# x for the sums on the GpSimd queue behind a pause of the weight sums, and the first dilated head beside them

## The chip, the core and the metric

The kernel runs on one core of a Trainium2 chip. Such a core has a matrix engine (TensorE, PE in the profile; its weight loads are PEld), a vector engine (VectorE, DVE), an engine for activations (ScalarE, ACT), a general engine (GpSimd, POOL) and an engine that mainly issues transfers (SyncE, SP). Each works through its own list of instructions in order and waits for the others by semaphores. SP and POOL each issue transfers (DMAs); the profile calls SP's queue `hardware_dynamic` (q1) and POOL's `software_dynamic` (q0). The metric is the device time of one execution in microseconds (us); smaller is better.

## What is computed

One layer of a decoder in float32 on x (512 tokens, 1024 channels). With `proj = x @ w_in`, cut into queries, keys, values and gates of three branches:

```python
o_da = diff_attention(...)            # 4 heads
o_sb = stick_breaking_attention(...)  # 8 heads
o_dl = dilated_attention(...)         # 3 groups x 4 heads: (window, dilation) = (128,1), (512,4), (2048,16)
g = jax.nn.sigmoid(gates).reshape(B, S, N_BRANCHES, D)
merged = (g[:, :, 0] * (o_da @ w_branch_da) + g[:, :, 1] * (o_sb @ w_branch_sb)
          + g[:, :, 2] * (o_dl @ w_branch_dil))
m = merged @ w_out
x = layer_norm(DEEPNORM_ALPHA * x + m, ln1_g, ln1_b)
c = jnp.square(relu(x @ w_up)) @ w_down
ple = jax.nn.sigmoid(x @ w_ple_gate) * (p @ w_ple)
x = layer_norm(DEEPNORM_ALPHA * x + c + ple, ln2_g, ln2_b)
```

The three dilated groups of one head slot are joined by their softmax denominators, so a dilated head in the kernel handles one slot of all three groups.

## The kernel before

Every large product is made of three matmuls of rounded parts: a float32 tile is split in a high part (`h`, a cast on ScalarE, L213) and the rest (`l`, a subtraction on VectorE, L215), and high x high, high x low and low x high are added up in PSUM. The weights come from HBM by SP in chunks of 512 KB (`raw`, seven buffers), are split into `wh` and `wl` (six buffers each), and are used by PE.

*Items.* The main stream is a list of items, each some 12 to 24 matmuls into one PSUM bank (`mm_bank`, two banks, or `at_bank`, six), and an eviction on ScalarE or VectorE when the next item has begun. Items 1 to 32 and 47 to 64 are projections (`t_item` and `v_items`; dl_v of group 0 is items 19 to 22, da_v 47 to 50), 65 to 72 the stick-breaking branch product (`branch_items(1)`), then gates, the other branches, `wout_items`, the layer norm and the MLP. Items 33 to 46 are the *value pair* (`value_pair`): the values of dilated groups 1 and 2 by a Strassen-like scheme with seven products, in the order 2, 1, 7, 6, 4, 5, 3, each in two halves r = 0, 1 of 12 matmuls. Half 0 of the first four or five products uses an `mm` bank, the others `at` banks. The scheme needs sums of weights and sums of x.

*Sums of weights* are made by the DMA engines alone, from HBM to HBM, with accumulating transfers issued on GpSimd (`sum_steps`, L1021; `vsum` for the value pair, `msum` for the gates, `bsum`, `gsum`, `usum`, `dsum` for later stages). How many steps an item emits is its `rate` x `size`, saved up as a credit (L1954 to L1960). A step waits for `marks[0]`, the fourth last entry of a list into which every split of a weight chunk (L218) and the evictions of `v_items` (L473) put their instruction; so a step runs no earlier than a VectorE instruction a few splits back. GpSimd issues in order: a step that waits holds all behind it.

*Sums of x* for the value pair come from `value_forms` (L345), a generator that begins at item 29: eight tiles `xr` of 256 KB are loaded on SP (L349), each after the last split emitted so far; VectorE then makes form 7 (L372), 6 (L365), 4 and 5 (L390), each split into high and low part (`split`, L239 on ScalarE, L240 on VectorE; u7h and u7l for form 7). `mixer_forms` (L513, begun at item 64) does the same for the gates, with eight loads in `load_xr` (L333).

*Heads.* Attention heads are generators too. `step()` (L1886), called once or twice in each item, moves every active head one `yield` on and starts waiting ones if PSUM banks suffice. Eight stick-breaking heads come first (`sb_head`), and only when none is active the first dilated head (`dil_head`, L1731). This makes logits of group 0 (matmuls L1749, bias and maximum L1752, exponent L1758), then of groups 1 and 2 (L1765, L1773, L1780), joins the denominators across rows (small matmuls L1790 and L1792 up to L1812, with an exponent L1807 on ScalarE), scales its maps (L1814, L1818), transposes them on PE (L1833, L1842) and multiplies them by the values (L1854, L1859). Head 0 waits with the whole of this until form 5 of `value_forms` is made (L1737), and takes two idle steps before its transposes (L1821).

Where an engine's instructions end up in its list is decided by a scheduler that goes by these dependences and the order of emission; engines run that list in order.

Of the kernel before, what the change touches and what calls it, by code (L numbers as in the profile page):

```python
# [55 lines left out]
def trunk(tc, a, out):  # L56
    nc = tc.nc
    es = ExitStack()
    with es:
# [14 lines left out]
        def slot(name, dt=F32):  # L74
            return big.tile([P, 512], dt, name=nm(name), tag="s", bufs=NSLOT)
# [63 lines left out]
        marks = deque(maxlen=4)  # L139
# [13 lines left out]
        def chunk(src, w):  # L153
            return chunk_of(load(src, w))
# [77 lines left out]
        items = []  # L232
# [14 lines left out]
        xt = a["xT"]  # L247
# [45 lines left out]
        def first_item():  # L293
# [19 lines left out]
            def ev(ps):  # L313
# [7 lines left out]
        vf = {p: [[(xh[k][:, 2 * th + r::4], xl[k][:, 2 * th + r::4]) for r in range(2)] for k in range(ks, ks + 4)]  # L321
              for p, ks, th in ((1, 0, 0), (2, 4, 0), (3, 4, 1))}
# [3 lines left out]
        def load_xr():  # L326

            r = {}
            for h in range(2):
                for th in range(2):  # L330
                    for kp in range(2):
                        t = slot("xr")
                        i = nc.sync.dma_start(t.rearrange("p (k t) -> p k t", k=2),  # L333
                                                xt[:, 4 * h + 2 * kp:4 * h + 2 * kp + 2, 256 * th:256 * th + 256])
                        tc.add_manual_dep(getattr(i, "ins", i), lows[-1].name, mybir.DependencyInfo(
                            mybir.DependencyClass.Sync, mybir.DependencyReason.DATA), reason="not ahead of time")
                        r[h, th, kp] = t
            return [[r[h, th, kp] for kp in range(2)] for h in range(2) for th in range(2)]
# [6 lines left out]
        def value_forms():  # L345

            xr = [slot("xr") for _ in range(8)]
            for k, t in enumerate(xr):
                i = nc.sync.dma_start(t, xt[:, k, :])  # L349
                tc.add_manual_dep(getattr(i, "ins", i), lows[-1].name, mybir.DependencyInfo(  # L350
                    mybir.DependencyClass.Sync, mybir.DependencyReason.DATA), reason="not ahead of time")

            def blk(kh, k, th):
                return xr[4 * kh + k].rearrange("p (t c) -> p c t", c=4)[:, 2 * th:2 * th + 2, :]

            def new():
                ts = [slot("fr") for _ in range(2)]
                return ts, [ts[k // 2].rearrange("p (k c t) -> p k c t", k=2, c=2)[:, k % 2] for k in range(4)]

            def parts(p, ts):  # L360
                form(vf, p, ts)
                vf[p] = [[(h[:, r * P:r * P + P], lo[:, r * P:r * P + P]) for r in range(2)] for h, lo in vf[p]]

            def neg_sub(o, i, j):
                nc.vector.scalar_tensor_tensor(o, i, -1.0, j, op0=OP.mult, op1=OP.subtract)  # L365

            for _ in range(WAIT):
                yield
            f7, o7 = new()
            with tc.issue_after(st["low"]):  # L370
                for k in range(4):
                    nc.vector.tensor_sub(o7[k], blk(1, k, 1), blk(0, k, 1))  # L372
            parts(7, f7)
            yield
            f6, o6 = new()
            with tc.issue_after(st["low"]):
                for k in range(4):
                    neg_sub(o6[k], o7[k], blk(0, k, 0))
            yield
            parts(6, f6)  # L380
            yield
            f4, o4 = new()
            for k in range(4):
                neg_sub(o4[k], o6[k], blk(1, k, 0))
            yield
            parts(4, f4)
            yield
            f1, o1 = new()
            for k in range(4):
                nc.vector.tensor_sub(o1[k], blk(0, k, 0), blk(0, k, 1))  # L390
            yield
            parts(5, f1)
            yield
# [53 lines left out]
        def v_items(nv, name, g):  # L447
            cs = [chunk(a["wv"][nv, c].rearrange("p k n -> p (k n)"), 1024) for c in range(4)]
            for tt in range(4):
                def mm(ps, tt=tt):  # L450
                    for k in range(8):
                        c = cs[k // 2]
                        s = slice((k % 2) * 512, (k % 2) * 512 + 512)
                        x1, x2 = xh[k][:, tt * P:tt * P + P], xl[k][:, tt * P:tt * P + P]
                        nc.tensor.matmul(ps, x1, c["h"][:, s], start=k == 0, stop=False)  # L455
                        nc.tensor.matmul(ps, x1, c["l"][:, s], start=False, stop=False)  # L456
                        nc.tensor.matmul(ps, x2, c["h"][:, s], start=False, stop=k == 7)  # L457
                        if k == 3:
                            yield

                def ev(ps, tt=tt):
                    if name == "sb_v":
                        v = [slot(name, F32R).rearrange("p (h two d) -> p h two d", two=2, d=64) for _ in range(2)]
                        pv = ps.rearrange("p (h d) -> p h d", d=64)
                        for i in range(2):
                            hs = slice(4 * i, 4 * i + 4)
                            nc.scalar.copy(v[i][:, :, 0, :], pv[:, hs, :])
                            nc.vector.tensor_sub(v[i][:, :, 1, :], pv[:, hs, :], v[i][:, :, 0, :].bitcast(F32))
                        V[name, g, tt] = v
                    else:  # L470
                        t = slot(name)
                        i = nc.vector.tensor_copy(t, ps)
                        marks.append(getattr(i, "ins", i))  # L473
                        marks.append(getattr(i, "ins", i))
                        V[name, g, tt] = t
                item(cs if tt == 3 else [], mm, ev, need=cs)
                items[-1]["rate"] = 2.5

        nt, nv = 2, 0
        order = main_order()  # L480
# [160 lines left out]
        def branch_items(i):  # L641
            for half in range(2):
                cs = [chunk(a["wb"][i - 1, half, c].rearrange("p k n -> p (k n)"), 1024) for c in range(2)]
                for tt in range(4):
                    def mm(ps, tt=tt, cs=cs):
                        q = slice(tt * P, tt * P + P)
                        for k in range(4):
                            c = cs[k // 2]
                            n = slice(k % 2 * 512, k % 2 * 512 + 512)
                            h, lo = oTs[4 * i + k]  # L650
                            nc.tensor.matmul(ps, h[:, q], c["h"][:, n], start=k == 0, stop=False)
                            nc.tensor.matmul(ps, h[:, q], c["l"][:, n], start=False, stop=False)
                            nc.tensor.matmul(ps, lo[:, q], c["h"][:, n], start=False, stop=k == 3)

                    def ev(ps, tt=tt, half=half):
                        if i == 1:
                            t = slot("b1")
                            nc.scalar.copy(t, ps)
                            merged[tt, half] = t
                            return  # L660
                        g = sg.pop((i, tt, half))
                        nc.vector.tensor_mul(g, g, ps)
                        nc.vector.tensor_add(merged[tt, half], merged[tt, half], g)

                    def pre(tt=tt, half=half):
                        sg[i, tt, half] = gate_sig(i, tt, half)
                    item(cs if tt == 3 else [], mm, ev, need=cs, bank=None if i == 1 else at_bank, size=0.5)
                    items[-1]["rate"] = 1.4
                    if i != 1:
                        items[-1]["pre"] = pre  # L670

# [93 lines left out]

        last_plain = len(items)
        for j, it in enumerate(items):
            it.setdefault("rate", 2.5 if j < 45 else 1.9)
        def first_gate(tt, half):
            g = gate_sig(1, tt, half)  # L770
            nc.vector.tensor_mul(merged[tt, half], merged[tt, half], g)
# [959 lines left out]
        def dil_head(hd):  # L1731
# [2 lines left out]

            while hd == 1 and ("dl_v", 1, 3) not in V:
                yield
            while hd == 0 and 5 not in vf:  # L1737
                yield
            q = [T["dl_q", 4 * g + hd] for g in range(3)]
            k = [T["dl_k", 4 * g + hd] for g in range(3)]  # L1740
            stt = one.tile([P, 2, 8], F32, name=nm("st"), tag="st", bufs=4)
# [76 lines left out]
                nc.vector.tensor_scalar(o, o, mxx[:, c:c + 1], None, op0=OP.mult)  # L1818
            yield

            for _ in range(2 if hd == 0 else 0):  # L1821
                yield

            src0 = {}
# [4 lines left out]
            for half in range(2):  # L1829
# [4 lines left out]
                t = slot("pt0")  # L1834
# [4 lines left out]
            for g in range(2):  # L1839
# [4 lines left out]
                t = slot("pt12")  # L1844
# [69 lines left out]
        for n, it in enumerate(items):  # L1914
# [63 lines left out]
            if n == ln2_at[0]:  # L1978

                i = nc.scalar.activation(small("rt", 1), ident[:, 0:1], AF.Sqrt)  # L1980
# [8 lines left out]
            ps = it["bank"]() if it["bank"] else mm_bank()  # L1989
# [113 lines left out]
```

## Time and profile before

| | us |
|---|---|
| runs of the kernel before | 1066.92, 1066.62, 1065.95; median 1066.62 |
| profiled execution | 1068.65, span of its instructions 1066.9 |

| engine | busy us | share of the span |
|---|---|---|
| PE | 1039.9 | 97% |
| PEld | 883.7 | 83% |
| DVE | 778.8 | 73% |
| ACT | 589.7 | 55% |
| POOL | 167.5 | 16% |

The profile is of one execution. A group's row has the source line, the engine, the operation, what it writes and reads, the count, and times. A row of the list of waits names the waiting instruction, what released it, the total, how often, and the longest. A row of the timeline has start, length, the instruction, and in brackets the idle time of its engine before it with the releaser. A row of the chain has start, length and what ran or was waited for. A window's row has the busy time of each engine in a stretch, the share of full clock that PE was granted, and the mean busy share of the 16 DMA engines. Line numbers are those of the kernel before; in the changed kernel they are one higher from L659 to L1736 and one lower from L1739 on.

### The profile page before, as it was taken

How to read it: one execution, taken by the hardware profiler on the slowest of the kernel's cores; microseconds unless marked ns; L12 is line 12 of the kernel's file. 1: busy time of each engine (PE TensorE's matmuls, PEld its weight loads, DVE VectorE, ACT ScalarE, POOL GpSimd, SP SyncE). 2: the span in 40 equal slices, each digit the busy share in tenths (PEclk: the TensorE clock that was granted, in tenths of full speed). 3: DMA queues.
4: the chain of work that ended last, by engine and by line, in shares of the span. 5: the costliest groups of instructions: out<-in, count | busy, mean ns of one | idle time of the engine just before them, and what ended most of it. 6: DMA issues, size and time to landing. Idle time of an engine off the chain costs nothing.

```text
span 1066.9 us, 15075 instructions
## 1 busy us (share of the span) xinstructions
PE 1039.9 (97%) x5462; PEld 883.7 (83%) x5462; DVE 778.8 (73%) x1392; ACT 589.7 (55%) x1006; POOL 167.5 (16%) x259
## 2 busy tenths in 40 slices
PE   9999999997799999999999999999999999999996
PEld 6887788876588888888888888888999989989885
DVE  6888667636865754878866786789677877877966
ACT  6666545514534544667672663585765565666641
POOL 0012312300020311101211122111211111111000
PEclk9999999998899999999999999999999999999999
DMA  8348977995494996837998998369999989989612
GB/s 311 115 159 260 216 214 231 303 303 148 136 287 123 280 269 200 233 113 261 277 351 261 340 313 288 115 206 325 303 334 339 337 275 328 301 290 289 196 39 80
DMA packets 76394, 260.09 MB, mean 244 GB/s; under 512 B 9144, under 2 KB 12104, under 8 KB 76320
## 3 DMA queue, kind: packets, MB, share of 16 engines
q0 software_dynamic: 32336, 116.21, 41.7%
q1 hardware_dynamic: 43408, 142.01, 36.8%
q8 instruction: 43, 0.70, 0.3%
q10 hardware_dynamic: 576, 0.92, 0.2%
q14 instruction: 31, 0.25, 0.1%
HBM read 256.98 MB, written 111.17 MB: 345 GB/s over the span
## 4 chain that ended last, share of the span: by engine, by line
PE 88%; DVE 4%; DMA 3%; ACT 2%; issue 2%; SPq 0%; POOL 0%; DVEq 0%; POOLq 0%
PE mm L87 9%; PE mm L89 9%; PE mm L88 9%; PE at L1211 4%; PE at L1212 4%; PE at L1213 4%; PE at L558 3%; PE at L560 3%; PE at L559 3%; PE mm L455 2%; PE mm L457 2%; PE mm L456 2%; DMA xr<-in_xT_dram 2%; PE at L89 1%; PE at L88 1%
## 5 line engine op out<-in xcount | busy, mean ns | idle before, releaser
L215 DVE TENSOR_TENSOR wl<-raw,wh 128x1024 fp32r<-128x1024 f32 x254 | 309.1, 1222 | 127.7 <-ACT wh L213 125.5
L213 ACT CAST wh<-raw 128x1024 fp32r<-128x1024 f32 x254 | 265.9, 1049 | 237.9 <-PE mm L88 127.2
L87 PE MATMUL mm<-xhT,wh 128*128 128x512 f32 x304 | 121.1, 398 | 0.0
L89 PE MATMUL mm<-xhT,wl 128*128 128x512 f32 x304 | 119.1, 392 | 0.0
L88 PE MATMUL mm<-xlT,wh 128*128 128x512 f32 x304 | 118.8, 391 | 0.0
L1211 PE MATMUL at<-wh,hh 128*128 128x512 f32 x188 | 73.7, 392 | 0.0
L1212 PE MATMUL at<-wl,hh 128*128 128x512 f32 x188 | 73.7, 392 | 0.0
L87 PE MATMUL mm<-x1hT,wh 128*128 128x256 f32 x256 | 73.6, 288 | 0.1
L1213 PE MATMUL at<-wh,hl 128*128 128x512 f32 x188 | 73.1, 389 | 0.0
L88 PE MATMUL mm<-x1lT,wh 128*128 128x256 f32 x256 | 72.2, 283 | 0.0
L89 PE MATMUL mm<-x1hT,wl 128*128 128x256 f32 x256 | 71.8, 283 | 0.0
L89 PEld LDWEIGHTS mm<-xhT,wl 128*128 128x128 f32 x304 | 57.1, 188 | 12.4 <-DVE wl L215 0.2
L87 PEld LDWEIGHTS mm<-xhT,wh 128*128 128x128 f32 x304 | 57.2, 188 | 11.5 <-issue 0.4
L88 PEld LDWEIGHTS mm<-xlT,wh 128*128 128x128 f32 x304 | 57.2, 188 | 10.6
L87 PEld LDWEIGHTS mm<-x1hT,wh 128*128 128x128 f32 x256 | 48.8, 190 | 4.7 <-ACT up L1145 2.8
L88 PEld LDWEIGHTS mm<-x1lT,wh 128*128 128x128 f32 x256 | 48.8, 191 | 1.5
L89 PEld LDWEIGHTS mm<-x1hT,wl 128*128 128x128 f32 x256 | 48.6, 191 | 0.0
L1048 POOL DMA_DIRECT2D usum<-in_wu_dram x32 | 26.9, 896 | 115.9 <-DVE wl L215 90.1
L1213 PEld LDWEIGHTS at<-wh,hl 128*128 128x128 f32 x188 | 35.3, 188 | 7.6
L1048 POOL DMA_DIRECT2D msum<-in_wgm_dram x24 | 21.3, 927 | 126.1 <-DVE wl L215 61.6
L1211 PEld LDWEIGHTS at<-wh,hh 128*128 128x128 f32 x188 | 35.5, 189 | 6.0
L1212 PEld LDWEIGHTS at<-wl,hh 128*128 128x128 f32 x188 | 35.5, 189 | 5.6
(604 smaller groups left out, 2671.7 us busy)
## 6 DMA issues: line engine op xcount, KB each, us to landing
usum<-in_wu_dram POOLq DMA_DIRECT2D x48, 512.0 KB, 8.8
dsum<-in_wd_dram POOLq DMA_DIRECT2D x42, 512.0 KB, 9.0
raw<-in_wt_dram SPq DMA_DIRECT2D x38, 512.0 KB, 5.2
msum<-in_wgm_dram POOLq DMA_DIRECT2D x36, 512.0 KB, 10.4
raw<-usum SPq DMA_DIRECT2D x32, 512.0 KB, 8.0
raw<-dsum SPq DMA_DIRECT2D x28, 512.0 KB, 7.1
raw<-in_wd_dram SPq DMA_DIRECT2D x25, 512.0 KB, 5.1
raw<-msum SPq DMA_DIRECT2D x24, 512.0 KB, 8.9
```

Of the source, the lines that this page charges most:

```text
L87: nc.tensor.matmul(ps, wh, xh, start=start, stop=False, skip_group_check=True)
L88: nc.tensor.matmul(ps, wh, xl, start=False, stop=False, skip_group_check=True)
L89: nc.tensor.matmul(ps, wl, xh, start=False, stop=stop, skip_group_check=True)
L213: i = nc.scalar.copy(h, raw)
L215: i = nc.vector.tensor_sub(lo, raw, h.bitcast(F32))
L558: nc.tensor.matmul(ps, h[:, q], c["h"][:, n], start=go, stop=False, skip_group_check=True)
L559: nc.tensor.matmul(ps, h[:, q], c["l"][:, n], start=False, stop=False, skip_group_check=True)
L560: nc.tensor.matmul(ps, lo[:, q], c["h"][:, n], start=False, stop=end, skip_group_check=True)
L1048: i = nc.gpsimd.dma_start(o, i, accum_op=OP.add, max_dma_last_dim=4096)
L1211: nc.tensor.matmul(ps, h[:, q], c["h"][:, s], start=go, stop=False, skip_group_check=True)
L1212: nc.tensor.matmul(ps, h[:, q], c["l"][:, s], start=False, stop=False, skip_group_check=True)
L1213: nc.tensor.matmul(ps, lo[:, q], c["h"][:, s], start=False, stop=end, skip_group_check=True)
```

## The change

Both sets of x loads are issued on GpSimd's queue in place of SP's. The rates change: projections up to item 24 emit 2.8 sum steps in place of 2.5, items of `v_items` 3.2 in place of 2.5, items 25 to 30 none, items 31, 32 and the rest as before; `branch_items(1)` 2.4 x 0.5 in place of 1.4 x 0.5. The evictions of `branch_items(1)`, on ScalarE, enter the list of marks. Dilated head 0 no longer waits for form 5, and takes six idle steps in place of two before its transposes.

```diff
@@ load_xr
-                        i = nc.sync.dma_start(t.rearrange("p (k t) -> p k t", k=2),
+                        i = nc.gpsimd.dma_start(t.rearrange("p (k t) -> p k t", k=2),
                                                 xt[:, 4 * h + 2 * kp:4 * h + 2 * kp + 2, 256 * th:256 * th + 256])
@@ value_forms
-                i = nc.sync.dma_start(t, xt[:, k, :])
+                i = nc.gpsimd.dma_start(t, xt[:, k, :])
@@ v_items
-                items[-1]["rate"] = 2.5
+                items[-1]["rate"] = 3.2
@@ branch_items
                         if i == 1:
                             t = slot("b1")
-                            nc.scalar.copy(t, ps)
+                            e = nc.scalar.copy(t, ps)
+                            marks.append(getattr(e, "ins", e))
...
-                    items[-1]["rate"] = 1.4
+                    items[-1]["rate"] = 2.4 if i == 1 else 1.4
@@ trunk
-            it.setdefault("rate", 2.5 if j < 45 else 1.9)
+            it.setdefault("rate", 2.8 if j < 25 else 0.0 if j < 31 else 2.5 if j < 45 else 1.9)
@@ dil_head
             while hd == 1 and ("dl_v", 1, 3) not in V:
                 yield
-            while hd == 0 and 5 not in vf:
-                yield
...
-            for _ in range(2 if hd == 0 else 0):
+            for _ in range(6 if hd == 0 else 0):
                 yield
```

## The prediction

> **What bounds the kernel now.** I read the engine totals, then the table of windows (where TensorE, PE, is not full), then the list of PE's waits inside the one stretch that stands out, then the chain of waits and the timeline there. The windows have the columns PE, PEld, DVE, ACT and POOL busy, granted clock, DMA share, GB/s.
>
> ```profile
> PE 1039.9 (97%) x5462; PEld 883.7 (83%) x5462; DVE 778.8 (73%) x1392; ACT 589.7 (55%) x1006; POOL 167.5 (16%) x259
> 100.00:200.00 100.00, 100.00 (x480) 80.99 (x480) 68.22 (x117) 48.06 (x77) 28.98 (x43) 1.00 0.87 239
> 215.00:238.20 23.20, 23.19 (x109) 19.08 (x107) 6.87 (x11) 4.66 (x7) 1.86 (x3) 1.00 1.05 298
> 238.20:302.56 64.36, 49.58 (x211) 42.82 (x212) 46.25 (x100) 28.83 (x49) 5.70 (x9) 0.87 0.58 171
> ```
>
> PE is full nearly everywhere (27 us idle in the span); 238.20 to 302.56 is the exception, with 14.8 us of that and a clock of 0.87. That is the fourteen half products of the value pair (products 2, 1, 7, 6, 4, 5, 3, two halves each) with dilated head 0. PE's waits there, and the rows around them:
>
> ```profile
> PE mm L422 <- ACT dl_q L287: 8.4, 1, 8.4
> PE at L1833 <- DVE L L1814: 4.9, 1, 4.9
> PE at L1790 <- DVE r L1783: 1.1, 1, 1.1
> PE mm L422 <- ACT dl_v L429: 0.4, 1, 0.4
> 246.63 0.81 PE L422 MATMUL mm<-wh,xhT 128*128 128x512 f32 x1 [8.44 <-ACT dl_q L287]
> 251.81 0.40 PE L422 MATMUL at<-wh,xhT 128*128 128x512 f32 x1
> 285.10 1.73 PE L1833 MATMUL at<-ident,L 128*128 128x128 f32 x7 [4.92 <-DVE L L1814]
> 291.35 0.47 PE L422 MATMUL at<-wh,u5h 128*128 128x512 f32 x1
> 302.56 1.68 PE L1854 MATMUL at<-pt,dl_v 128*128 128x256 f32 x8
> ```
>
> After the first wait twelve matmuls take 251.81 - 246.63 = 5.18 us; 48 later ones (291.35 to 302.56) take 11.21, 0.2335 each. So twelve cost 2.80 and the slow restart lost 2.4 us. The second restart loses about 1.9 (six matmuls of 0.43 instead of 0.23, transposes at half speed). Lost in all: 8.4 + 2.4 + 0.4 + 1.1 + 4.9 + 1.9 = 19.1 us.
>
> The chain of waits (start, length) says why the first wait is there:
>
> ```profile
> 215.07 8.46 DMA raw<-in_wv_dram
> 223.60 20.05 DMA xr<-in_xT_dram
> 243.75 0.62 DVE fr L372
> 244.91 1.04 ACT wh L213
> 245.98 0.61 ACT dl_q L287
> ...
> 215.45 8.48 SPq L349 DMA_DIRECT2D xr<-in_xT_dram  x8
> DMA to landing us min/median/max: 11.3/18.9/22.3
> ```
>
> The last of the eight x tiles lands at 243.65. VectorE (DVE) stands in order before fr L372, ScalarE (ACT) before the cast of fr, and the eviction dl_q that frees PE's bank is queued behind that cast: PE resumes 3.0 us after x. The second wait is DVE's: from 266 to 285 it makes forms, splits and head 0's softmax back to back while PE has nothing else.
>
> The issues between 206 and 221 tell why x is slow (median us to landing at the end of each), against sums on a quiet queue at 74 to 90 and four 256 KB table loads at 292.6:
>
> ```profile
> msum<-msum POOLq DMA_DIRECT2D x4, 512.0 KB, 22.7
> xr<-in_xT_dram SPq DMA_DIRECT2D x7, 256.0 KB, 18.0
> ...
> msum<-in_wgm_dram POOLq DMA_DIRECT2D x3, 512.0 KB, 5.8
> ...
> L1444 POOL DMA_DIRECT2D sh<-rv x4: 746/758/790, 292.6 to 294.2; - x4
> DMA to landing us min/median/max: 8.3/9.4/10.5
> ```
>
> The DMA engines are full (1.05 in the window 215 to 238), and a sum took four times as long as on the quiet queue.
>
> **The change part by part.**
>
> *Rates.* Counting the credit item by item, before the change 52 sum steps are emitted by item 32, after it 42; 37 of them by item 24 (before 32), none at items 25 to 30, and steps 38 to 40 at item 31, tied to the VectorE split that released a step at 208.58. In the new order of the GpSimd queue exactly 40 steps stand before the x loads. Before, step 33 was released at 171.8, and step 52 went out at 219.6, with x:
>
> ```profile
> 171.77 0.52 POOL L1050 DMA_DIRECT2D msum<-in_wgm_dram  x1 [12.26 <-DVE wl L215]
> 208.58 0.81 POOL L1048 DMA_DIRECT2D msum<-in_wgm_dram  x1 [3.63 <-DVE wl L215]
> 219.63 0.52 POOL L1050 DMA_DIRECT2D msum<-msum  x1 [1.90 <-DMA msum<-in_wgm_dram]
> 213.81 1.23 DVE L215 TENSOR_TENSOR wl<-raw,wh 128x1024 fp32r<-128x1024 f32 x1 [0.17 <-ACT wh L213]
> 226.89 1.23 DVE L215 TENSOR_TENSOR wl<-raw,wh 128x1024 fp32r<-128x1024 f32 x1 [0.17 <-ACT wh L213]
> 230.06 0.58 ACT L1641 COPY ot<-at 64x512 f32<-64x512 f32 x1 [3.21 <-PE at L1635]
> ```
>
> (The last three rows are for the next parts.) Those twelve go behind x. I estimate that steps 33 to 37 land by about 190, and the three of 208.6, at the quiet 5.8 us and a little more for each behind the first, by about 217. The steps made earlier lie at 100 to 172, where PE has no idle time (the row of 100 to 200), so they cost nothing; without that cover a late weight load would stop PE.
>
> *The first eight x loads.* They still wait for the same split (213.81 + 1.23 = 215.04), so they start no earlier than on SP. An issue takes GpSimd 0.52 to 0.79 us, eight of them 4.2 to 6.3; the last leaves at 219 to 223.6 (on SP it left then, and PE may hold its slot as long). With 5.8 to 10.5 us to landing the last x is there at 225 to 234. I take 229, since the table loads are of x's size and 8.3 to 10.5 came with two weight loads beside them. Behind them on GpSimd wait sum steps 41 to 43, needed much later. On SP the eight issues, 8.48 us, vanish, so two weight loads that stood at 226.8 and 230.0 go out as their buffers come free.
>
> *What x at 231 gives.* VectorE's queue reaches fr at 226.89 + 1.23 = 228.1 and has to wait for head 7's copy until 230.06 + 0.58 = 230.6 in any case, so x up to 231 costs nothing, and two or three us beyond are slack of the steps that follow. dl_q is then out near 235, before PE needs the bank at 238.2: the 8.4 and the 2.4 go.
>
> *Head 0 beside the sums.* Removing the wait on form 5 moves its logits (L1749 before the first product, L1765 after it) and its softmax to the front, and six idle steps instead of two put the transposes (L1833) eight half products behind the logits; before it was six. Durations that I use:
>
> ```profile
> L213 ACT CAST wh<-raw 128x1024 fp32r<-128x1024 f32 x11 | 11.5, 1049 | 5.5 <-PE at L424 3.3 <-PE mm L88 1.9 <-PE mm L424 0.2
> 306.03 1.52 PE at L1749 x8
> 310.30 1.78 PE at L1765 x16
> 332.31 0.76 PE at L1833 x7
> 335.82 0.87 PE at L1842 x8
> ```
>
> PE's own work: 168 matmuls x 0.2335 = 39.2, and 1.5 + 1.8 + 0.8 + 0.9 and about 0.4 for the two small folds = 5.4 for head 0: 44.6. New waits, followed through the new order of each engine: a weight buffer comes free six chunks back, so ACT's cast for product 5 stands until product 7 is done (258.7), and behind it on ACT stand head 0's exponent, one more cast, and the copy (0.6, as dl_q above) that frees the bank of product 6: 258.7 + 1.05 + 0.25 + 1.05 + 0.6 = 261.7 where PE is ready at 260.6, 1.2 lost with the signal. In the same way the cast for product 3 stands until product 6 is done (265.5), then 1.05 and two copies: 267.8 where PE is ready at 266.1, 1.8 lost. VectorE scales head 0's maps by about 264.4, before PE transposes at 265.5. Together 238.2 + 44.6 + 3.0 = 285.8 against 302.56: **16.8 us**. If these two waits do not come it is 19 to 20; if each is doubled, 14.
>
> Gaps of 1.2 and 1.8 us keep the clock, as the 1.1 us wait at L1790 did. The Trainium skill (TensorE: Matmul & The Clock Gate, What's actually happening) has a lower price for the long gaps: about 3.4 us at half speed after an idle window, so by my estimate 1.7 us lost per restart. With that the sum would be 15.9; the trace measured 2.4 and 1.9, and these stand.
>
> *The second eight x loads* (mixer_forms). On GpSimd they queue behind sum steps and wait for slots as they did on SP; their users come late:
>
> ```profile
> L333 SPq DMA_DIRECT2D xr<-in_xT_dram x8: 419/422/3532, 441.6 to 445.7; - x8
> L521 DVE TENSOR_TENSOR xr<-xr,xr x2: 683/683/683, 465.5 to 466.1; 128x512 f32<-128x512 f32 x2
> ```
>
> They have 20 us where 10.5 was the longest of the table loads: nothing, with -1 (SP is not held 3.5 us) and +3 as ends.
>
> *Later rates, marks on ACT's copies.* At the end of the first branch items the sums are 2.7 steps behind. Cover: the branch sums are complete long before they are read.
>
> ```profile
> L1048 POOL DMA_DIRECT2D bsum<-in_wbq_dram x4: 807/825/867, 350.8 to 426.4; - x4
> L183 SPq DMA_DIRECT2D raw<-bsum x4: 320/323/326, 593.9 to 604.5; - x4
> ```
>
> 2.7 steps, at 22.7 us each even, are 61 of these 167 us: nothing. One more sum step now stands between the layer norm's small GpSimd operations; it waits for an earlier split: 0 to +3.
>
> The profiled execution took 1068.65 us (span 1066.9), 2 above the median 1066.62. Its sum is 1068.65 - 16.8 = 1051.9; against the median I predict **1049.8**.
>
> **The rivals.**
>
> *The other queue brings nothing.* If sums still fill the engines, x lands near 243.7 again, on whichever queue. Then 8.4 + 2.4 stay and only 4.9 + 1.9 + 1.1 + 0.4 = 8.3 go: 1058.3. For it: the sums depend on VectorE's splits, not on items, and could bunch later; this would also be the case in which the pause does not do what it says. Against it: only three steps are released after 172 and before 215. Chance 0.14. The Trainium skill (DMA: Bandwidth & Descriptors, Issuing engines are not separate DMA queues) states this rule: DMAs of all engines run on the same 16 DMA engines, and another issuer saves only issue time. The trace agrees as far as xr on SP took 18 to 22 us beside the sums' queue; by the rule alone the move is worth nothing and the pause everything.
>
> *ACT and VectorE become the bound.* VectorE has 46.25 us of work in the stage of 64.36; in 47.6 it is nearly full, and each cast that waits on PE holds head 0's exponent. Three more waits of 1.5: 1054. Chance 0.09.
>
> *Slower.* The x loads are held at GpSimd: each waits until the eighth DMA before it has landed, and sums took 22.7 us to land. If the steps of 208.3 land at 235, loads 6 to 8 go out there. PE would start at landing + 3 and needs 47.6, so the change loses from a landing after 252 on (302.56 - 47.6 - 3). A landing at 260 gives 1074.6. It needs 25 us after 235, which only sums in full contention took. Chance 0.10, with what small waits may add elsewhere.
>
> **How the numbers follow.** Forecast 0.62, the two partial rivals 0.23, no change 0.05, slower 0.10; 0.2% (2.1 us) is about what a measurement of this kernel tells from no change. Faster 0.85, same 0.05, slower 0.10. The range goes from 1046 (gain of 20.5, no new waits) to 1060 (x late, and a little lost elsewhere): it leaves out the last two and the edges of the first.
>
> **What the profile after would show.** The wait at the first L422 gone; xr landing within about 10 us, by about 231; the stage from the first product to head 0's L1854 at 47 to 49 us and no clock below 0.95 in it; PE's waits there on ACT's copies, 1 to 2 us each; the sum steps 41 and on after x; nothing new after 345. Wrong would be: fr L372 still waiting for x beyond 238, a long wait of PE at L1790 or L1833, or GpSimd's x issues starting after 216.

## The result, and the profile after

The changed kernel takes 1047.80 us (median of 5 runs, 1047.52 to 1048.12) against 1066.62 before: 18.8 us less, a ratio of 0.9824 with a 95% interval of 0.981 to 0.9839. Its profiled execution took 1047.8 us, with a span of 1046.0.

The engine totals of the profile after, then three rows of its table of windows, cut at the same points of the work as before the change: the stretch of 100 to 200, the time beside the x loads, and the stage of the value pair with head 0.

```profile
PE 1034.0 (99%) x5462; PEld 881.1 (84%) x5462; DVE 777.9 (74%) x1392; ACT 588.6 (56%) x1006; POOL 179.2 (17%) x275
```

```profile
100.00:200.00 100.00, 100.00 (x480) 81.23 (x480) 68.84 (x119) 47.97 (x77) 23.47 (x35) 1.00 0.86 229
215.00:237.15 22.15, 22.15 (x105) 18.50 (x105) 14.37 (x22) 8.57 (x13) 6.28 (x11) 1.00 0.90 260
237.15:281.78 44.63, 44.63 (x212) 40.11 (x211) 37.52 (x89) 24.14 (x44) 7.02 (x10) 1.00 0.63 176
```

The stage went from 64.36 us with a clock of 0.87 to 44.63 us with a clock of 1.00, and PE is busy in all of it. That is 19.7 us. The list of PE's waits in the whole span has nothing of this stage any more; these are its four longest rows:

```profile
PE at L1390 <- DVE zero L1387: 1.3, 1, 1.3
PE at L310 <- ACT wh L213: 0.8, 1, 0.8
PE at L131 <- ACT da_ka L122: 0.8, 2, 0.6
PE at L131 <- ACT da_kb L124: 0.3, 1, 0.3
```

GpSimd's timeline around the x loads, the view of the x line with its times to landing, and the row of PE that ends the stage:

```profile
207.69 1.53 POOL L1051 DMA_DIRECT2D msum<-in_wgm_dram  x3 [33.48 <-DVE wl L215]
214.45 4.27 POOL L349 DMA_DIRECT2D xr<-in_xT_dram  x8 [5.23 <-DVE wl L215]
219.16 1.75 POOL L1049 DMA_DIRECT2D msum<-in_wgm_dram  x2 [0.44 <-DMA xr<-in_xT_dram]
```

```profile
DMA to landing us min/median/max: 4.4/5.7/6.1
```

```profile
281.78 1.68 PE L1853 MATMUL at<-pt,dl_v 128*128 128x256 f32 x8
```

GpSimd is idle for 33.5 us before the three steps of 207.69 (the pause), the x loads go out in 4.3 us, and each lands 4.4 to 6.1 us later, the last one at 224.3 (218.2 + 6.1). Before the change it landed at 243.65.

The two profiled executions are 1068.65 - 1047.80 = 20.85 us apart. Of this 19.7 is the stage, and about 1 us was there before it: PE reached the stage at 237.15 in place of 238.20. The first rows of the windows of both profiles (before, then after) show that this came in the first 100 us, where nothing is changed that PE waits for:

```profile
0.00:100.00 100.00, 97.85 (x448) 76.49 (x449) 79.86 (x147) 64.82 (x105) 9.60 (x23) 1.00 0.61 209
```

```profile
0.00:100.00 100.00, 97.90 (x452) 76.90 (x452) 80.26 (x148) 65.67 (x106) 10.74 (x24) 1.00 0.64 214
```

Four matmuls more, at 0.23 each, are 0.9 us. In the run with only the queue moved, which has the rates of before, PE came to the stage at 237.04 (244.10 - 7.06), and the profiled execution of before was 2.0 us above its median; so this is part of the spread of the runs and no gain of the change. From the stage's end to the span's end it is 764.3 us before and 764.2 after.

### The profile page after: what moved, and what is told of

It reads as the page before. It is cut to its first block, busy times and chain, and to the rows that moved or that the text cites. A ratio compares the mean times of both kernels' runs of the same rounds, so it can differ in the third digit from the quotient of the medians.

```text
span 1046.0 us, 15082 instructions
## 1 busy us (share of the span) xinstructions
PE 1034.0 (99%) x5462; PEld 881.1 (84%) x5462; DVE 777.9 (74%) x1392; ACT 588.6 (56%) x1006; POOL 179.2 (17%) x275
## 4 chain that ended last, share of the span: by engine, by line
PE 96%; ACT 2%; DVE 1%; DMA 0%; issue 0%; SPq 0%; DVEq 0%
PE mm L87 10%; PE mm L89 10%; PE mm L88 10%; PE at L1212 4%; PE at L1213 4%; PE at L1214 4%; PE at L558 3%; PE at L560 3%; PE at L559 3%; PE mm L455 2%; PE mm L457 2%; PE mm L456 2%; PE at L89 1%; PE at L87 1%; PE at L88 1%; PE at L849 1%
## 5 line engine op out<-in xcount | busy, mean ns | idle before, releaser
L1049 POOL DMA_DIRECT2D dsum<-in_wd_dram x28 | 24.1, 881 | 94.5 <-DVE wl L215 67.9
```

Of the source, the lines that this page charges most:

```text
L1049: i = nc.gpsimd.dma_start(o, i, accum_op=OP.add, max_dma_last_dim=4096)
```

## The experiments

The change has three parts that can be set one by one: the queue of the first eight x loads (SP or GpSimd), the rates with the pause, and head 0. All eight combinations are in this table; the ratio is to the kernel before in the same session (its median was 1066.62, 1067.75 and 1066.87 in the sessions of the table). Runs that take a part back hold the small parts (the second eight x loads, the marks, the rate of 2.4), runs that add a part to the kernel before do not; the last experiment takes the first two of these back.

| queue | rates | head 0 | run | us (median) | ratio, 95% interval |
|---|---|---|---|---|---|
| SP | before | before | the kernel before | 1066.62 | |
| GpSimd | before | before | e6_only_queue | 1065.36 | 0.9974 to 0.9993 |
| SP | pause | before | e5_only_pause | 1056.88 | 0.9893 to 0.9922 |
| SP | before | changed | e4_only_head | 1056.40 | 0.9878 to 0.9911 |
| GpSimd | pause | before | e3_head_back | 1056.37 | 0.9883 to 0.9913 |
| GpSimd | before | changed | e1_no_pause | 1055.76 | 0.9876 to 0.9906 |
| SP | pause | changed | e2_x_on_sp | 1047.58 | 0.98 to 0.9829 |
| GpSimd | pause | changed | the changed kernel | 1047.80 | 0.981 to 0.9839 |

**The queue alone taken back.** The changed kernel with the first eight x loads on SP.

```diff
-                i = nc.gpsimd.dma_start(t, xt[:, k, :])
+                i = nc.sync.dma_start(t, xt[:, k, :])
```

> The changed kernel with the first eight x loads back on SP; the pause, the rates and head 0 stay. PE, VectorE and ScalarE have the same order as in the changed kernel. Theory 1 (the pause empties the DMA engines and the queue hardly matters): x starts at 214 on SP as well and lands by 225 to 232, still before the 231 up to which nothing is lost; PE stays full; 1047.8, at most 1 us more for the weight loads that stand behind x on SP. Theory 2 (GpSimd's queue is what brings x early): x lands near 243 again and the 8.4 + 2.4 us come back: 1058.

1047.58 us, the same as the changed kernel within their spread. The view of the x line:

```profile
L349 SPq DMA_DIRECT2D xr<-in_xT_dram x8: 328/428/557, 214.5 to 218.2; - x8
DMA to landing us min/median/max: 3.9/12.3/12.8
```

On SP the loads run beside the next sum steps (issued at 214.3, 214.9 and 220.5, since x no longer stands ahead of them) and take 12.3 us in place of 5.7. The last lands at 231.0, the edge that the prediction gave for what costs nothing. Theory 1 holds: given the pause, the queue is worth 6.7 us of landing time (231.0 against 224.3) and no time of the kernel.

**The pause taken back.** x on GpSimd and head 0 as changed, the rates of before.

```diff
-            it.setdefault("rate", 2.8 if j < 25 else 0.0 if j < 31 else 2.5 if j < 45 else 1.9)
+            it.setdefault("rate", 2.5 if j < 45 else 1.9)
...
-                items[-1]["rate"] = 3.2
+                items[-1]["rate"] = 2.5
```

> The changed kernel with the rates of the kernel before (no pause, 52 sum steps ahead of x on GpSimd's queue in place of 40); x on GpSimd and head 0 as changed. Theory 1: x stands behind steps issued until 219.6 which took 22.7 us each to land, and lands at 245 to 255; PE starts the value pair about 3 us after that and restarts slowly (2.4): with 44.6 us of PE work in the stage, of which 1.5 is done before the wait, that is 1058 to 1068. Theory 2 (the queue matters, not the sums): x lands by 231 and the time is 1048.

1055.76 us: neither theory. The pause matters (8 us), but x lands at 239.8, not at 245 to 255. GpSimd's timeline says how (the last sum step ahead of the loads, then the first, fourth, fifth and last load), and PE's list of waits what it costs:

```profile
211.44 0.54 POOL L1051 DMA_DIRECT2D msum<-msum  x1 [2.69 <-DMA msum<-in_wgm_dram]
215.28 0.56 POOL L349 DMA_DIRECT2D xr<-in_xT_dram  x1 [3.31 <-DMA msum<-in_wgm_dram]
...
224.28 0.54 POOL L349 DMA_DIRECT2D xr<-in_xT_dram  x1 [2.18 <-DMA msum<-in_wgm_dram]
227.77 0.54 POOL L349 DMA_DIRECT2D xr<-in_xT_dram  x1 [2.96 <-DMA msum<-in_wgm_dram]
...
234.78 0.54 POOL L349 DMA_DIRECT2D xr<-in_xT_dram  x1 [2.02 <-DMA msum<-msum]
```

```profile
PE mm L422 <- ACT dl_q L287: 4.7, 1, 4.7
PE at L1390 <- DVE zero L1387: 1.3, 1, 1.3
PE mm L651 <- DVE da_klb L101: 1.1, 1, 1.1
```

The loads are held at GpSimd, each until a sum issued eight transfers earlier has landed (the sum of 196.57 landed at 214.72, and the first load went out at 215.28), as the prediction's slower rival had it. But while they are held no further sum is issued, and the last load takes 5.0 us in place of 19.9 for the first. 4.7 + 1.1 and a slow restart of 2.9 (twelve matmuls and the first five of head 0's logits behind them in 6.3 us in place of 3.4) make 8.7, beside 8.6 between the two profiled executions (1056.4 and 1047.8) and 8.0 between the medians.

**Head 0 taken back.** Queue and pause as changed, head 0 as before.

```diff
+            while hd == 0 and 5 not in vf:
+                yield
...
-            for _ in range(6 if hd == 0 else 0):
+            for _ in range(2 if hd == 0 else 0):
```

> The changed kernel with head 0 waiting for form 5 again, and two idle steps: the queue and the pause stay. PE's order is that of the kernel before. Theory 1 (two separate causes): x lands at 224 as in the changed kernel, the first wait of 8.4 and its slow restart of 2.4 stay away, and the later losses return, 4.9 + 1.9 + 1.1 + 0.4 = 8.3: 1056.1. Theory 2 (with x early VectorE gets ahead, and the later waits go too): 1048 to 1050.

1056.37 us, 8.6 above the changed kernel; theory 1, to 0.3 us. PE's waits are those of before without the first:

```profile
PE at L1834 <- DVE L L1815: 4.9, 1, 4.9
PE at L1390 <- DVE zero L1387: 1.3, 1, 1.3
PE at L1791 <- DVE r L1784: 1.1, 1, 1.1
```

x at 224 does not let VectorE get ahead: head 0's maps are late because the head starts late.

**Only head 0.** The kernel before with that edit alone.

> The kernel before with only the change of head 0 (no wait for form 5, six idle steps). PE's order is that of the changed kernel. Theory 1: x lands at 243.7 on SP, the value pair starts at 246.6 and restarts slowly, but head 0's 1.5 us of first logits lie ahead of the wait: 246.6 + 43.1 + 2.4 = 292.1 in place of 302.56, so 1056 (up to 1060 if VectorE, which then has forms and head 0 at once, is late). Theory 2 (the two parts only work together, since VectorE's forms come late and now have head 0 in front of them): no gain, 1066 or more.

1056.40 us, theory 1 (1056). x lands at 243.2, PE waits 7.1 at the first product and restarts slowly (1.6 lost); its list of waits has nothing else in the stage. Without the pause, too, PE waits there for x and for no late weights.

**Only the rates.** The kernel before with the pause and the rates 2.8 and 3.2. In this run the sums stay four steps behind the changed kernel's to the end, because the 2.4 of the first branch items is missing, and one of the last sums is read before its last step is added (the step of 974.35 stood behind the read of 966.5). So the kernel's result is wrong; all transfers and matmuls are executed, and none of this lies in the stage, so the time can be used.

> The kernel before with only the changed rates of the sum steps (2.8, 3.2 and the pause); x on SP, head 0 as before. Theory 1 (pause and head are separate causes and the queue is worth nothing with the pause): x lands by about 231, the wait of 8.4 and its slow restart of 2.4 go and the later losses of 8.3 stay: 1056.4, as with the run that only took head 0 back. Theory 2 (without the early head the queue matters, since VectorE has no head to do and waits for x): 1058 to 1062.

1056.88 us: theory 1 (1056.4). x lands at 231.0 on SP, the first wait is gone, 4.9 and 1.1 stay.

**Only the queue.** The kernel before with the first eight x loads on GpSimd.

> The kernel before with only the first eight x loads on GpSimd; 52 sum steps stand ahead of them. The run without the pause showed x held there until the sums landed, the last at 239.8, 3.9 us earlier than on SP, since no sums are issued behind them meanwhile. Theory 1 (that repeats here): PE's first wait shrinks from 8.4 by 3 to 4 and everything else stays: 1063 to 1064. Theory 2 (the early landing there came from head 0's place): x lands at 243 or later and the time is 1066 to 1070.

1065.36 us, a gain of 1.5 in the session's own pair (1066.87). x lands at 240.6, 3.0 earlier than before, but the wait shrinks by 1.4 only, from 8.44 to 7.06: PE resumes at 244.1, 3.5 us after x, and it had come to the wait 1.1 us earlier in this execution. Theory 1 had the direction and twice the size.

**x issued later.** The changed kernel with the loads emitted two and three items later, the forms at their place.

```diff
             xr = [slot("xr") for _ in range(8)]
+            for _ in range(2):
+                yield
             for k, t in enumerate(xr):
...
-            for _ in range(WAIT):
+            for _ in range(WAIT - 2):
```

> The changed kernel with the first eight x loads issued two items later, behind a split that ends at about 227 in place of 214. Theory 1 (only x's landing decides, nothing is lost up to 231 and little up to 234): x lands at about 237, fr follows at once, PE waits 1 to 3 us at the first product, too short to slow its clock, and head 0's work is unchanged: 1049 to 1051. Theory 2 (forms and head 0 are so tight on VectorE that a shift of 12 us in x is lost again further on): 1054 or more.

> The changed kernel with the first eight x loads issued three items later, behind a split that ends at about 234. Theory 1: x lands at about 243, where it landed before the change, with an empty queue; the value pair starts at 246 as it did before, with 1.5 us of head 0 done ahead; a wait of 7 and a slow restart of 2.4: 1057, as the run with only head 0 changed. Theory 2 (the traffic beside x costs by itself, through late weights): better than that run by 2 or more, since the engines are free here.

1048.19 and 1048.71 us. The split that they wait for was the next one (220.3), not one at 227 or 234, so the landings were missed: 231.5 and 234.6. At those landings the times answer the question all the same. At 231.5 PE has no wait in the stage; the 0.4 above the changed kernel stands in waits at L310, in the first 20 us of the span (1.7 in place of 0.8). At 234.6 the kernel takes 0.9 more, of which the trace shows 0.6 as a wait of PE at L1791. The second was meant to put x at 243 on empty engines; that was not tried again, so whether the traffic beside x costs anything by itself was not tested in that way.

**x issued earlier.** The kernel before with the change of head 0, no pause, x on SP but emitted two items earlier.

```diff
-            v_from[0] = len(items) - 4
+            v_from[0] = len(items) - 6
...
-        WAIT = 5
+        WAIT = 7
```

> The kernel before with the change of head 0, its rates as before (no pause), and x on SP but emitted two items earlier; the forms stay at their place. The sums fill the engines as before. Theory 1 (only x's landing counts): x starts by about 208 in place of 215 and takes 18 to 22 us beside the sums, landing at 228 to 235; the first wait is 0 to 1 and the time 1048 to 1050. Theory 2 (x cannot start earlier, since its slots come free late, or the sums only delay it more): x lands at 240 or later, and the time is 1055 to 1057.

1056.12 us. x starts at 201.9 and lands at 234.9: beside the sums the loads take 13 to 27 us, with a median of 21.5 against 18.4 in the run with only head 0 changed, where they start at 214.8. And the wait went to another place. The times to landing from the view of the x line, and the first row of PE's waits:

```profile
DMA to landing us min/median/max: 13.2/21.5/26.8
```

```profile
PE mm L87 <- DVE dl_k L289: 5.1, 1, 5.1
```

The scheduler now puts the subtractions fr ahead of the copy dl_k that frees a projection's bank; they wait for x, and the copy behind them. A landing at 234.6 cost 0.9 us behind the pause, and one at 234.9 cost 5.1 and a restart here. What counts is the landing against fr's place in VectorE's order, so theory 1 fell in that form. The time lies in theory 2's range, but not for its reason: x landed within the 228 to 235 of theory 1.

**Head 0's idle steps.** The changed kernel with two of them in place of six.

> The changed kernel with two idle steps of head 0 ahead of its transposes, as before the change, in place of six. In PE's order the first transposes stand after 60 matmuls of the value pair in place of 96, so PE comes to them 36 x 0.2335 = 8.4 us earlier, at about 255. Theory 1 (the idle steps are needed): VectorE scales the maps only after the exponent that followed the two folds, by about 260 to 261; PE waits 4 to 6 us and restarts slowly (1 to 2): 1053 to 1056. Theory 2 (what matters is only that head 0 starts ahead of the products): 1048.

1053.48 us, theory 1: 5.7 above the changed kernel. The rows of PE's timeline where the transposes now stand:

```profile
259.03 1.73 PE L1832 MATMUL at<-ident,L 128*128 128x128 f32 x7 [3.54 <-DVE L L1813]
260.41 0.77 PE L422 MATMUL at<-wh,u7h 128*128 128x512 f32 x1
...
264.39 0.58 PE L422 MATMUL at<-wh,u7h 128*128 128x512 f32 x1
264.81 0.40 PE L423 MATMUL at<-wl,u7h 128*128 128x512 f32 x1
```

A wait of 3.5, seven transposes that take 1.4 us in place of 0.8, and ten matmuls that take 4.4 in place of 2.3: the six idle steps are worth as much as two thirds of the head's part.

**Two more copies on ScalarE**, behind the copy that frees the bank of product 6.

```diff
                             nc.scalar.copy(s[1, r], ps)
+                            if r == 0:
+                                nc.scalar.copy(s[1, r], ps)
+                                nc.scalar.copy(s[1, r], ps)
```

> The changed kernel with two more copies of 0.58 us on ScalarE behind the copy L433 that frees the bank of product 6, with the same result. In the changed kernel that copy ended at 259.64 and PE began the product at 259.72. Theory 1 (the wait of 1.2 that was forecast there missed only by its start: the cast ahead waits for half a product, not for the whole, and the slack is nearly zero): PE waits 0.8 to 1.1 us there, 1048.6 to 1049. Theory 2 (there is slack of a microsecond or more): no wait, 1047.8.

1048.87 us, 1.1 above the changed kernel: the size of theory 1 at another place. The scheduler put the first half of product 6 behind the first transposes, and PE waits there for VectorE's maps (L1816 in this run):

```profile
261.50 0.60 PE L1835 MATMUL at<-ident,L 128*128 128x128 f32 x3 [1.06 <-DVE L L1816]
```

So the edit cost 1.1 through the changed order of PE; whether the copy of product 6 itself had any slack stays open.

**The small parts.** The second eight x loads back on SP, and ScalarE's copies out of the list of marks. The rate of 2.4 stayed in this run, contrary to what the expectation says, and no sum step is left out.

> The changed kernel with the second eight x loads (mixer_forms) back on SP, the evictions of the first branch items not in the list of marks, and their rate 1.4 in place of 2.4; by the last it leaves out the last two or three steps of the sums. Theory 1 (these parts cost and bring nothing): 1047.8, within 1. Theory 2 (SP is held by the eight issues, or the sums of the gates come late): 1 to 3 more, with waits of PE between 420 and 480.

1047.76 us, no new wait of PE. On SP these loads take 7 to 16 us to land in place of 5.8; the last is there at 441.1, 3.4 us before VectorE first uses them (444.5): theory 1.

## Why the prediction was right

The mechanism was right in its main parts, the early x and the early head, and one term, 3.0 us of new waits, was not there. 1047.80 lies in the range, 2.0 below the 1049.8. Against its own execution the sum said 1051.9 and the profile after says 1047.8: 4.1 off, 3.0 of it from one term and about 1 from the later start of the profiled execution of before.

*What was lost before.* The split of 19.1 us in two causes holds. Pause alone gives 9.7 to 10.0 us (predicted 8.4 + 2.4 = 10.8), head 0 alone 10.2 to 11.4 (predicted 8.3), both together 18.8; the two ends are taken from the medians of the kernel before in two sessions. The single parts add up to more than the whole since, with head 0 alone, the wait for x is also 1.3 shorter (head 0's first logits, 1.5 us, run ahead of it) and the restart behind it 0.8 cheaper. One reading was too broad: from 266 to 285 PE is not without work, it is busy 12.75 of these 19 us, and only the last 4.9 are the wait.

*The rates and the first x loads.* 40 steps stand ahead of x. The three of 208 landed at 215.3 (predicted 217). The first load left at 214.45, and x landed at 224.3 where 229 was taken from a range of 225 to 234: less ran beside it than beside the table loads (two weight loads in place of five, the DMA engines busy 0.91 of the time in place of 0.99), and GpSimd sent no sum until x was out. So the landing was 4.7 us off, and it made no difference, as up to 231 was free: in the runs with x at 231.0 and 231.5 PE has no wait in the stage, and the one at 234.6 shows the slack behind it.

*Head 0 beside the sums.* PE's work of 44.6 us in the stage was measured as 44.63. The step that failed is the one on new waits: 1.2 us for product 6 and 1.8 us for product 4, both put down to ScalarE's order. Neither came. The stage took 44.6 us where 47 to 49 were forecast, and PE's waits of 1 to 2 us on ScalarE's copies were not there. ScalarE's rows of the profile after, and PE's row that was to wait, for product 6:

```profile
256.74 1.06 ACT L213 CAST wh<-raw 128x1024 fp32r<-128x1024 f32 x1 [2.37 <-PE at L424]
257.70 0.21 ACT L1806 ACTIVATE ex<-ex 128x16 f32<-128x16 f32 x1
258.10 1.06 ACT L213 CAST wh<-raw 128x1024 fp32r<-128x1024 f32 x1 [0.19 <-PE at L424]
259.06 0.58 ACT L433 COPY dl_v<-mm 128x512 f32<-128x512 f32 x1
259.72 0.48 PE L422 MATMUL mm<-wh,u6h 128*128 128x512 f32 x1
```

The order is as predicted, and the casts do wait for product 7. But a product has two weight chunks, and the first cast needs only the first one free: it ran at 256.74, while PE was still in the second chunk. Only the second cast waited for the product's end (258.1). So one cast and the exponent, 1.05 + 0.25, lay beside PE's work and not behind it, and the copy ended at 259.64, just ahead of PE. For product 4 it is the same:

```profile
261.39 1.06 ACT L213 CAST wh<-raw 128x1024 fp32r<-128x1024 f32 x1 [0.71 <-PE mm L424]
262.35 0.58 ACT L433 COPY dl_v<-at 128x512 f32<-128x512 f32 x1
262.82 0.59 ACT L429 COPY dl_v<-mm 128x512 f32<-128x512 f32 x1
263.94 0.48 PE L422 MATMUL mm<-wh,u4h 128*128 128x512 f32 x1
```

The cast ahead of the two copies needed the first chunk of product 6 and ran at 261.39, while PE was still in that product; the copy that frees the bank ended at 263.41, 0.5 us ahead of PE. The term of 3.0 measured 0. The prediction's other bound, a gain of 19 to 20 without these waits, is what the stage shows.

*Terms put at nothing.* The later x loads and the marks cost nothing, as taken: from the stage's end on, both profiles take 764.2 to 764.3 us. The rates after the pause are no idle detail: without the 2.4 the sums end four steps later, and one of the last is read too early.

*The rivals.* That the other queue brings nothing was right in one half: with the pause the move is worth nothing, and the pause is what brings x early. This is the rule that the prediction took from the Trainium skill (DMA: Bandwidth & Descriptors, Issuing engines are not separate DMA queues), and the runs agree with it as far as the time goes. Without the pause the queue did count, by 3 us of landing and 0.6 to 1.5 us of time (1055.76 against 1056.40, 1065.36 against 1066.87), because GpSimd issues in order and also holds back the sums behind x (none went out between 211.4 and 235.5). The slower rival's mechanism is real, loads held at GpSimd until sums have landed, but it needs the sums ahead that the pause takes away, and even with them x came at 240 and not at 252, the point from which it loses. ScalarE and VectorE did not become the bound: VectorE has 37.5 us of work in 44.63. The 46.25 us that the rival counted did not all stay in the stage: in the 22 us ahead of it VectorE's work rose from 6.9 to 14.4, since with x early VectorE makes the first sums of x there (L372 from 228.3 on, L365 from 234.4 on).

## What to carry to other kernels

When a small load is late behind bulk transfers, look first for what keeps the DMA engines full at that moment and stop issuing it for a while (here GpSimd was idle for 33.5 us); which engine issues the load is second. When two waits follow each other on the full engine, list what each waits for: here each had its own cause, each part of the change removed one, and either alone gave half. For a forecast of buffer waits, count in the unit in which buffers are freed (a chunk, not a product).

## What was not expected of the hardware

A wait of PE of 3.5 us already brought the slow phase (waits of 1.1 us, as at L1790, did not, and no run has one between 1.3 and 3.5, so whether the 1.8 us of the prediction would have kept the clock is not shown), and its length differs for waits of like length. After 8.4 us twelve matmuls ran at the low speed; in the run with only head 0 changed the wait was 7.1 us and the slow phase ended after seven:

```profile
246.15 0.81 PE L422 MATMUL mm<-wh,xhT 128*128 128x512 f32 x1 [7.13 <-ACT dl_q L287]
246.76 0.63 PE L423 MATMUL mm<-wl,xhT 128*128 128x512 f32 x1
...
249.32 0.46 PE L423 MATMUL mm<-wl,xhT 128*128 128x512 f32 x1
249.62 0.40 PE L424 MATMUL mm<-wh,xlT 128*128 128x512 f32 x1
```

Eight matmuls in 3.5 us in place of 1.9 are 1.6 us lost, against 2.4 before, 2.9 after the wait of 4.7 in the run without the pause, and 2.7 after the wait of 3.5 in the run with two idle steps (transposes and matmuls together). So the price of a restart was 1.6 to 2.9 us here and did not grow with the wait, and a difference of a microsecond between two kernels with such a wait says nothing. The slow phases lasted 3.5 to 6.3 us. The Trainium skill (TensorE: Matmul & The Clock Gate, What's actually happening) says that the window by which the clock is set is free-running, which would fit the spread; its length there, about 3.4 us, is near the shortest slow phase here and does not by itself give the longer ones. No run here shows the window.

The same x loads of 256 KB took 5.7 us (median) on a paused GpSimd queue, 12.3 on SP beside three sums, 18.4 to 18.9 on SP beside the full stream of sums, and 21.5 when issued earlier into that stream.
